# First sub-layer of a two-layer trunk: the first modulation group in two halves, squares of one token tile moved to VectorE

## The chip, the core and the metric

The kernel runs on one NeuronCore of one Trainium2 chip, as one launch. The metric is the device time of the launch in microseconds (us), a median over several runs. The engines are TensorE (PE in the profile, with its weight loads as PEld), VectorE (DVE), ScalarE (ACT), GpSimd (POOL) and SyncE (SP), which issues most loads. Each engine works through its own list of instructions in order and waits at semaphores for the others.

## The reference, cut to what matters

128 context tokens and 256 latent tokens (three tiles of 128 tokens, width 1024) pass through two layers of three sub-layers each. The change is in the start of the first sub-layer alone:

```
m  = (silu(cond) @ mod_w[0] + mod_b[0]).reshape(9, 1024)       # shift = m[0], scale = m[1], for each of two conds
hf = rms_norm(x, g[0]) * (1 + scale) + shift
x  = x + 0.5 * m[2] * rms_norm((silu(hf @ w1g) * (hf @ w1u)) @ w2, g[1])     # w1: 1024 x 5632, w2: 2816 x 1024
```

`rms_norm(x)` needs the sum of squares of each token. `shift` and `scale` need 2048 columns of the modulation weights (8 MB in fp32). All later sub-layers take the same path, but their modulation is computed under the sub-layer before.

## The kernel before

Products in fp32 precision are made of three matmuls in a faster format: each operand is split into a high part and a low rest (`xh`, `xl` for the tokens, `whi`, `wlo` for weights), and `mm3` adds high by high, low by high and high by low (the three matmuls of L445 to L447, one after the other).

`start` holds the whole stretch that is changed. Its steps:

- The tokens arrive as three tiles of 0.5 MB, `x` tile 0, 1, 2. `stat_steps` gives for a tile two squares with an accumulated sum (ScalarE, L331, one for each half of 512 columns), a reciprocal root (a `Sqrt` on ScalarE, L309, and small VectorE steps, in `rstd_of`), and a scaled tile `xn` (half on VectorE, L384, half on ScalarE, L385).
- `transposed` turns `xn` into column blocks on TensorE (L391) and copies them to `xnT` (L765, one half on VectorE, one on ScalarE).
- The modulation vectors come in four groups g of 256 columns of shift and 256 of scale, that is of two column blocks k = 2g and 2g + 1 each. `load(g)` loads two tiles of 1 MB. `mods(g, v)` multiplies one by the conditioning in 8 small matmuls (L788), `rows` copies the result out of PSUM (L796), `vectors` transposes it by 4 matmuls with two columns (L801), and four VectorE instructions (L809, L811) add bias and norm weight.
- `evac(g)` applies scale and shift for both column blocks of a group: `xtmp` on VectorE (L840) and ScalarE (L842), then `xh` (ScalarE, L431) and `xl` (VectorE, L432).
- `products(g, u)` multiplies these blocks by the first three weight units u (gate and up columns, gus 0 and 1): 12 matmuls for a group and unit. Where a number of products is given below, each is one matmul of L445 to L447.

`keep_warm` runs matmuls on the identity with no use for the result; ten stand at the start, ten before the first `evac`. The instructions of this stretch run in the order in which the code emits them on each engine (`order_begin` fixes it). SyncE issues the loads in the order of the code, and a load waits until the eighth load before it has landed. After `start` comes the loop over the other weight units in `ffn`, and then the five further sub-layers; none of that is edited.

Of the kernel before, what the change touches and what calls it, by code (L numbers as in the profile page):

```python
# [26 lines left out]
RS = -0.5  # L27
# [4 lines left out]
HALF_BUFS = 3  # L32
WARM, WARM2 = 10, 10
TAIL = 5


class Trunk:
    def __init__(self, ctx, tc, io):
        self.ctx, self.tc, self.nc, self.io = ctx, tc, tc.nc, io
        nc = self.nc  # L40
# [21 lines left out]
        self.sel = const("sel", [P, 2])  # L62
        nc.gpsimd.dma_start(self.sel, io["sel"])
        self.csT = const("csT", [P, KC, 32])
        nc.vector.memset(self.csT, 0.0)
# [305 lines left out]
    def stat_steps(self, t):  # L371

        nc = self.nc
        st = {}

        square, eps, sums = self.square_steps([self.x[:, t, 0:512], self.x[:, t, 512:1024]])

        def rstd():
            eps()
            st["z"] = self.rstd_of(**sums)  # L380

        def scale(tag="xn"):
# [342 lines left out]
    def start(self, units):  # L725


        nc, io = self.nc, self.io
        with self.tc.tile_pool(name="start", bufs=1, reuse_waits="tile") as tp:
# [13 lines left out]

            load(0)
            for g in range(2):
                for u in range(3):
                    load_part(u, 512 * g, 512 * (g + 1))
                load(g + 1)
            load_part(0, D, 2 * D)
# [24 lines left out]
            def squares(t):  # L774
                for h in (1, 0):
                    stats[t][0](h)

            vec = [self.mod_vec(v) for v in range(2)]
            self.shift[0], self.scale[0] = vec
# [18 lines left out]
            def vectors(g, *vs):  # L798
                po = self.psum(1)
                for i in range(2 * vs[0], 2 * vs[-1] + 2):  # L800
                    nc.tensor.matmul(po[:, 2 * i : 2 * i + 2], rowsof[g][:, i * P : (i + 1) * P], self.sel,  # L801
                                     start=True, stop=True)
                for v in vs:
                    for j in range(2):
                        k = 2 * g + j
                        src = po[:, 4 * v + 2 * j : 4 * v + 2 * j + 2]
                        b = self.mbT[:, 0, v, k : k + 1]
                        if v == 0:
                            nc.vector.tensor_scalar(vec[0][:, :, k], src, b, None, op0=ALU.add)  # L809
                        else:  # L810
                            nc.vector.tensor_scalar(vec[1][:, :, k], src, b, self.nwT[:, 0, k : k + 1],  # L811
                                                    op0=ALU.add, op1=ALU.mult)

            squares(0), stats[0][1]()
            squares(1)
            xn0 = stats[0][2]()
            stats[1][1]()
            squares(2)
            xn1 = stats[1][2]("ptmp")
            nc.vector.tensor_scalar(self.nwT, self.nwT, RS, None, op0=ALU.mult)  # L820
            for j in range(6):
                nc.vector.tensor_scalar(self.mbT[:, j, 1, :], self.mbT[:, j, 1, :], 1.0, None, op0=ALU.add)
            stats[2][1]()
            transposed(0, xn0)
# [11 lines left out]
            def evac(g, between=None):  # L836
                for j in range(2):
                    k = 2 * g + j
# [11 lines left out]

            def products(g, u, gus=(0, 1)):
                for gu in gus:
                    for j in range(2):
                        k = 2 * g + j
# [494 lines left out]
def host_arrays(i):  # L1349
# [12 lines left out]
    first = np.asarray(i["mod_w"])[0, :, 0:2048].reshape(KC, P, 2, 4, 256)  # L1362
    a["mod_first"] = f(first.transpose(3, 2, 1, 0, 4))
    mb = np.asarray(i["mod_b"]).reshape(6, 3, D)
# [86 lines left out]
```

## Time and profile before

| | |
|---|---|
| median of 3 runs | 1422.34 us (1422.31 to 1422.74) |
| profiled execution, its own time | 1423.91 us |
| its span, first to last instruction | 1421.0 us |
| TensorE busy | 1405.4 us (99%) |
| VectorE, ScalarE, GpSimd busy | 1021.1, 614.5, 29.0 us |
| mean granted clock | 0.999 |

The span lies inside the execution's own time; the other 2.9 us are before the first and after the last instruction. A busy TensorE is one with a matmul in flight; at full rate the matmuls of L445 to L447 overlap each other.

### The profile page before, as it was taken

The page shows a single profiled execution, that of the slowest core. Times are in us where ns is not written, and L with a number is a line of the kernel's source. Part 1 is how long each engine was busy: PE and PEld are TensorE (multiplying, and loading weights), DVE is VectorE, ACT ScalarE, POOL GpSimd, SP SyncE. Part 2 cuts the span into 40 slices and gives each one's busy share as a digit, 9 for nine tenths or more (in the row PEclk, how much of TensorE's full clock was granted, in tenths as well). Part 3 has the DMA queues.
Part 4 walks back from the last instruction along what each step waited for, and adds up shares of the span by engine and source line. Part 5 has one row for each costly group of instructions (what it writes and reads, how often), then busy time and mean ns, then how long its engine had stood idle before and what let it go on. Part 6 is the DMA issues. An engine that isn't in the chain of part 4 may idle for free.

```text
span 1421.0 us, 19853 instructions
## 1 busy us (share of the span) xinstructions
PE 1405.4 (99%) x7747; PEld 1287.3 (91%) x7747; DVE 1021.1 (72%) x1798; ACT 614.5 (43%) x1051; POOL 29.0 (2%) x54
## 2 busy tenths in 40 slices
PE   8999999999999999999999999999999999999998
PEld 6999998889888999999889999988886899999886
DVE  5688868578997777986856889887678765555333
ACT  5533332363555633333355333323657663333322
POOL 0000000010000000000000000000100000000000
PEclk9999999999999999999999999999999999999999
DMA  9556555626545246655734566556350334444321
GB/s 372 212 214 259 195 207 221 260 100 247 201 149 199 96 175 235 237 207 182 275 135 153 203 233 241 198 217 251 107 205 30 119 119 152 173 150 178 130 107 45
DMA packets 38958, 262.58 MB, mean 185 GB/s; under 512 B 4816, under 2 KB 4976, under 8 KB 8784
## 3 DMA queue, kind: packets, MB, share of 16 engines
q1 hardware_dynamic: 35424, 243.29, 46.9%
q0 software_dynamic: 3440, 18.02, 3.5%
q8 instruction: 60, 0.98, 0.3%
q14 instruction: 34, 0.28, 0.1%
HBM read 259.01 MB, written 2.29 MB: 184 GB/s over the span
## 4 chain that ended last, share of the span: by engine, by line
PE 93%; DVE 3%; DMA 1%; ACT 1%; issue 1%; DVEq 0%; SPq 0%; ACTq 0%; POOLq 0%
PE psB L445 29%; PE psB L446 29%; PE psB L447 29%; PE psB L391 2%; PE psB L941 1%; PE psB L982 1%; DVE junkv L229 1%; DVE wlo L155 1%; DMA raw<-in_mod_w 1%; DMA csB<-crows 1%; PE psB L788 0%; ACT junk L331 0%; DMA x<-in_x_prompt 0%; PE psB L955 0%; PE psB L801 0%
## 5 line engine op out<-in xcount | busy, mean ns | idle before, releaser
L445 PE MATMUL psB<-xh,whi 128*128 128x384 f32 (+1 forms) x1536 | 517.0, 337 | 0.9 <-ACT qz L1085 0.7
L446 PE MATMUL psB<-xl,whi 128*128 128x384 f32 (+1 forms) x1536 | 512.3, 334 | 0.1
L447 PE MATMUL psB<-xh,wlo 128*128 128x384 f32 (+1 forms) x1536 | 512.0, 333 | 0.0
L155 DVE TENSOR_TENSOR wlo<-raw,whi 128x1024 fp32r<-128x1024 f32 (+2 forms) x286 | 336.6, 1186 | 121.0 <-ACT whi L152 119.2
L152 ACT CAST whi<-raw 128x1024 fp32r<-128x1024 f32 (+1 forms) x275 | 285.6, 1045 | 295.8 <-PE psB L446 132.2
L229 DVE CUSTOM_DVE_ANT_0 junkv<-raw,csB,mbT 128x1024 bf16<-128x1024 f32 x256 | 328.1, 1281 | 8.8 <-DMA csB<-crows 3.7
L445 PEld LDWEIGHTS psB<-xh,whi 128*128 128x128 f32 x1536 | 288.8, 188 | 5.7 <-issue 2.3
L446 PEld LDWEIGHTS psB<-xl,whi 128*128 128x128 f32 x1536 | 288.9, 188 | 1.6 <-DVE xl L432 0.9
L447 PEld LDWEIGHTS psB<-xh,wlo 128*128 128x128 f32 x1536 | 288.8, 188 | 0.0
L445 PE MATMUL psB<-whi,g 128*128 128x512 f32 x384 | 149.9, 390 | 0.0
L447 PE MATMUL psB<-whi,g 128*128 128x512 f32 x384 | 149.4, 389 | 0.0
L446 PE MATMUL psB<-wlo,g 128*128 128x512 f32 x384 | 149.4, 389 | 0.0
L431 ACT CAST g<-gt 128x384 fp32r<-128x384 f32 (+1 forms) x84 | 42.5, 505 | 201.3 <-DVE gt L622 201.3
L622 DVE TENSOR_TENSOR gt<-psB,sil 128x384 f32<-128x384 f32 (+1 forms) x88 | 48.1, 547 | 82.5 <-PE psB L447 74.7
L445 PEld LDWEIGHTS psB<-whi,g 128*128 128x128 f32 x384 | 72.1, 188 | 14.9
L447 PEld LDWEIGHTS psB<-whi,g 128*128 128x128 f32 x384 | 72.1, 188 | 14.9
L446 PEld LDWEIGHTS psB<-wlo,g 128*128 128x128 f32 x384 | 72.1, 188 | 14.7
L432 DVE TENSOR_TENSOR g<-gt,g 128x384 fp32r<-128x384 f32 (+1 forms) x84 | 46.1, 549 | 48.1 <-ACT g L431 48.1
L620 ACT ACTIVATE sil<-psB 128x384 f32<-128x384 f32 (+1 forms) x88 | 42.7, 485 | 86.5 <-PE psB L447 86.5
L445 PE MATMUL psB<-g,g 128*128 128x512 f32 x120 | 46.9, 391 | 0.0
L447 PE MATMUL psB<-g,g 128*128 128x512 f32 x120 | 46.7, 389 | 0.0
L446 PE MATMUL psB<-g,g 128*128 128x512 f32 x120 | 46.7, 389 | 0.0
(227 smaller groups left out, 1410.1 us busy)
## 6 DMA issues: line engine op xcount, KB each, us to landing
raw<-in_ffn_w SPq DMA_DIRECT2D x129, 1024.0 KB, 4.9
raw<-in_mod_w SPq DMA_DIRECT2D x64, 1024.0 KB, 4.9
raw<-in_ev_in SPq DMA_DIRECT2D x10, 1024.0 KB, 4.8
m<-in_mod_first SPq DMA_DIRECT2D x8, 1024.0 KB, 13.1
gate<-gscr POOLq DMA_DIRECT2D x6, 1024.0 KB, 5.0
csB<-crows POOLq DMA_DIRECT2D x4, 1024.0 KB, 7.4
raw<-in_ev_out SPq DMA_DIRECT2D x4, 1024.0 KB, 5.1
raw<-in_od_out SPq DMA_DIRECT2D x4, 1024.0 KB, 4.9
```

Source lines behind the costliest of these rows:

```text
L152: nc.scalar.copy(hi, src)
L155: sub = lambda hi=hi[:, c], lo=lo[:, c], src=src[:, c]: nc.vector.tensor_tensor(lo, src, hi.bitcast(F32), ALU.subtract)
L229: nc.vector.tensor_tensor_reduce(junk[:, :D], self.raw[i][0][:, kk * D : (kk + 1) * D], self.csB[:, c, :], 1.0, self.mbT[:, s, kind, k : k ...
L391: self.nc.tensor.transpose(out, src, self.ident)
L431: self.nc.scalar.copy(hi, src)
L432: sub = lambda: self.nc.vector.tensor_tensor(lo, src, hi.bitcast(F32), ALU.subtract)
L445: nc.tensor.matmul(out, ah, bh, start=first, stop=False)
L446: nc.tensor.matmul(out, ah, bl, start=False, stop=False)
L447: nc.tensor.matmul(out, al, bh, start=False, stop=last)
L620: nc.scalar.activation(sil[:, :n], pg[:, :n], AF.Silu)
L622: nc.vector.tensor_tensor(gt[:, :n], pu[:, :n], sil[:, :n], ALU.mult)
L941: nc.tensor.matmul(sp[:, :384], qk(i, e, t + 1), kk(i, e)[0], start=True, stop=True)
```

## The change

The group g = 0 is loaded as four tiles of 0.5 MB, one for each vector v (shift, scale) and column block j, and computed in two halves: `mods_half`, `rows_half` and `vectors_half` for block 0 stand ahead of the transposes of token tile 2; those for block 1 stand behind the first six products. `evac` and `products` take the column blocks of a group apart by `js`, and the order of products and of the groups 1 and 2 among them is new. The squares of token tile 1 go to VectorE (`square_dve`), with their own sum. Seven small VectorE instructions on norm weights and biases go to GpSimd. The second `keep_warm` is gone.

```diff
+        nc.gpsimd.tensor_scalar(self.nwT, self.nwT, RS, None, op0=ALU.mult)
+        for j in range(6):
+            nc.gpsimd.tensor_scalar(self.mbT[:, j, 1, :], self.mbT[:, j, 1, :], 1.0, None, op0=ALU.add)
...
-            load(0)
-            for g in range(2):
-                for u in range(3):
-                    load_part(u, 512 * g, 512 * (g + 1))
-                load(g + 1)
+            load_half(0)
+            load_part(0, 0, 512)
+            load_half(1)
+            load_part(1, 0, 512)
+            load_part(2, 0, 512)
+            load(1)
+            for u in range(3):
+                load_part(u, 512, 1024)
+            load(2)
...
+            def square_dve(h):
+                junk = self.cp.tile([P, D + 192], BF16, tag="junkv", name=self.name("junkv"))
+                xs = self.x[:, 1, 512 * h : 512 * h + 512]
+                nc.vector.tensor_tensor_reduce(junk[:, 0:512], xs, xs, 1.0 / D, zero, ALU.mult, ALU.add,
+                                               ss1[:, h : h + 1])
...
+            def mods_half(v, j):
+                if v == 0:
+                    sums[0, j] = self.psum(0)
+                for kk in range(2):
+                    for q in range(4):
+                        nc.tensor.matmul(sums[0, j][32 * q : 32 * q + 32, P * v : P * v + P],
+                                         self.csT[:, 2 * q + kk, :], raw0[0, v, j][:, 2 * q + kk, :],
+                                         start=(kk == 0), stop=(kk == 1))
...
-            squares(0), stats[0][1]()
-            squares(1)
+            squares(0), stats[0][3]()
+            square_dve(1)
+            stats[0][1]()
+            stats[2][0](1)
             xn0 = stats[0][2]()
-            stats[1][1]()
-            squares(2)
-            xn1 = stats[1][2]("ptmp")
-            nc.vector.tensor_scalar(self.nwT, self.nwT, RS, None, op0=ALU.mult)
-            for j in range(6):
-                nc.vector.tensor_scalar(self.mbT[:, j, 1, :], self.mbT[:, j, 1, :], 1.0, None, op0=ALU.add)
+            square_dve(0)
+            stats[2][0](0)
+            nc.vector.tensor_tensor(ss1[:, 0:1], ss1[:, 0:1], ss1[:, 1:2], ALU.add)
+            z1 = self.rstd_of(ss1[:, 0:1])
+            xn1 = stats[1][2]("ptmp", z1)
             stats[2][1]()
             transposed(0, xn0)
             xn2 = stats[2][2]()
             transposed(1, xn1)
-            mods(0, 0)
-            rows(0, 0)
+            mods_half(0, 0)
+            mods_half(1, 0)
+            rows_half(0)
+            vectors_half(0)
             transposed(2, xn2)
-            mods(0, 1)
             parts = {0: self.prep(1, "all")}
             parts[0][0]()
-            rows(0, 1)
...
-            vectors(0, 0, 1)
-            keep_warm(0, WARM2)
-            evac(0, parts[0][1])
+            evac(0, parts[0][1], (0,))
+            weights(0, 0)
+            products(0, 0, js=(0,))
+            mods_half(0, 1), mods_half(1, 1), rows_half(1)
             for u in (1, 2):
                 parts[u] = self.prep(1, "all")
                 parts[u][0](), parts[u][1]()
-            for u in range(3):
                 weights(u, 0)
-            products(0, 0)
-            products(0, 1)
+                if u == 1:
+                    vectors_half(1)
+                products(0, u, js=(0,))
+            evac(0, None, (1,))
+            products(0, 0, js=(1,))
             for u in range(3):
                 parts[u][2](), parts[u][3]()
             mods(1, 0), mods(1, 1), rows(1, 0, 1)
-            products(0, 2, (0,))
+            products(0, 1, js=(1,))
             vectors(1, 0, 1)
             evac(1)
-            products(0, 2, (1,))
+            products(0, 2, js=(1,))
+            products(1, 0, (0,))
             mods(2, 0), mods(2, 1), rows(2, 0, 1)
-            products(1, 0)
+            products(1, 0, (1,))
             vectors(2, 0, 1)
```

The host array `mod_first0` holds the first group in the new layout. Line numbers of the changed kernel are some 5 higher at the helpers (L445 to L447 become L450 to L452, L331 becomes L334), and 24 to 56 higher in `start`.

The order of instructions shows the change at three places. The first is ScalarE's list from the first square on, before; `ss_6`, `ss_7` and `ss_8` are the sums of token tiles 0, 1 and 2, and `xn_168` and `xn_186` the scaled tiles 0 and 1:

```order
L331 ACTIVATE junk_149,ss_6_133<-x 128x512
L331 ACTIVATE junk_151,ss_6_133<-x 128x512
L309 ACTIVATE rq_154<-ss_6_133 128x1
L331 ACTIVATE junk_164,ss_7_134<-x 128x512
L331 ACTIVATE junk_166,ss_7_134<-x 128x512
L385 ACTIVATE xn_168<-x,rz_161 128x512
L309 ACTIVATE rq_172<-ss_7_134 128x1
L331 ACTIVATE junk_182,ss_8_135<-x 128x512
L331 ACTIVATE junk_184,ss_8_135<-x 128x512
L385 ACTIVATE xn_186<-x,rz_179 128x512
L309 ACTIVATE rq_197<-ss_8_135 128x1
```

The same stretch of ScalarE's list in the changed kernel, where `xn_182` and `xn_200` are the scaled tiles 0 and 1, and `rv_191` the sum of tile 1 from VectorE:

```order
L334 ACTIVATE junk_163,ss_6_144<-x 128x512
L334 ACTIVATE junk_165,ss_6_144<-x 128x512
L312 ACTIVATE rq_170<-ss_6_144 128x1
L334 ACTIVATE junk_180,ss_8_146<-x 128x512
L390 ACTIVATE xn_182<-x,rz_177 128x512
L334 ACTIVATE junk_187,ss_8_146<-x 128x512
L310 ACTIVATE rq_190<-rv_191 128x1
L390 ACTIVATE xn_200<-x,rz_197 128x512
L312 ACTIVATE rq_204<-ss_8_146 128x1
```

The two squares of tile 1 are gone, and a square of tile 2 stands on either side of the scaling of tile 0, ahead of the root of tile 1.

The second place is TensorE's list around its first products, before; `psB_42` and `psB_43` take the transposes of token tile 2, `m_0_1` is the scale tile of group 0, and `psB_46` collects gate columns of unit 0:

```order
L391 MATMUL psB_42_245<-ident,xn_219 128x128 x4
L391 MATMUL psB_43_246<-ident,xn_219 128x128 x4
L788 MATMUL psB_40_234<-m_0_1_99,csT 32x256 x8
L801 MATMUL psB_52_275<-sel,rows_243 128x2 x4
L771 MATMUL psB_53_284<-ident 128x128 x10
L445 MATMUL psB_46_269<-xh,whi_265 128x384
L446 MATMUL psB_46_269<-xl,whi_265 128x384
L447 MATMUL psB_46_269<-xh,wlo_266 128x384
L445 MATMUL psB_46_269<-xh,whi_265 128x384
L446 MATMUL psB_46_269<-xl,whi_265 128x384
L447 MATMUL psB_46_269<-xh,wlo_266 128x384
```

The same place in the changed kernel, where `psB_44` and `psB_45` take the transposes of token tile 2, `m0h_1` are the two tiles of block 1 (shift, then scale), and `psB_48` and `psB_49` collect the gate and up columns of unit 0:

```order
L855 MATMUL psB_43_260<-sel,rows_258 128x2 x2
L396 MATMUL psB_44_265<-ident,xn_226 128x128 x4
L396 MATMUL psB_45_266<-ident,xn_226 128x128 x4
L450 MATMUL psB_48_280<-xh,whi_277 128x384
L451 MATMUL psB_48_280<-xl,whi_277 128x384
L452 MATMUL psB_48_280<-xh,wlo_278 128x384
L450 MATMUL psB_49_281<-xh,whi_277 128x384
L451 MATMUL psB_49_281<-xl,whi_277 128x384
L452 MATMUL psB_49_281<-xh,wlo_278 128x384
L844 MATMUL psB_56_300<-m0h_1_110,csT 32x128 x8
L844 MATMUL psB_56_300<-m0h_1_112,csT 32x128 x8
L855 MATMUL psB_60_323<-sel,rows_317 128x2 x2
```

The transposes of tile 2 moved behind the small matmuls of `vectors_half(0)`, and 16 small matmuls and two more of `vectors_half(1)` moved from ahead of the first product to behind the sixth.

The third place is TensorE's list behind the vectors of group 1 (the end of the products of group 0 and unit 2, then those of group 1), before; `m_2_0` and `m_2_1` are the tiles of group 2, and `psB_46` is the first bank that takes products of group 1:

```order
L447 MATMUL psB_51_274<-xh,wlo_311 128x384
L788 MATMUL psB_66_396<-m_2_0_114,csT 32x256 x8
L788 MATMUL psB_66_396<-m_2_1_116,csT 32x256 x8
L445 MATMUL psB_46_269<-xh,whi_265 128x384
L446 MATMUL psB_46_269<-xl,whi_265 128x384
L447 MATMUL psB_46_269<-xh,wlo_266 128x384
```

The same place in the changed kernel, with `psB_48` as the first bank of group 1's products:

```order
L452 MATMUL psB_53_285<-xh,wlo_335 128x384
L450 MATMUL psB_48_280<-xh,whi_277 128x384
L451 MATMUL psB_48_280<-xl,whi_277 128x384
L452 MATMUL psB_48_280<-xh,wlo_278 128x384
L450 MATMUL psB_48_280<-xh,whi_277 128x384
L451 MATMUL psB_48_280<-xl,whi_277 128x384
L452 MATMUL psB_48_280<-xh,wlo_278 128x384
L812 MATMUL psB_69_417<-m_2_0_125,csT 32x256 x8
```

Six products of group 1 moved from behind the 16 small matmuls of group 2 to ahead of them.

## Rows read from the trace of the kernel before

**Rows 1.** Stretches: length, busy PE, PEld, DVE, ACT, POOL, granted clock, DMA share, GB/s.

```profile
0.00:18.10 18.10, 12.65 (x104) 10.25 (x105) 9.12 (x39) 13.44 (x30) 2.97 (x10) 1.00 0.89 333
...
20.20:37.90 17.70, 17.70 (x148) 15.00 (x147) 8.95 (x23) 7.09 (x13) 0.00 (x0) 1.00 1.01 414
```

**Rows 2.** Timeline, ScalarE: start, duration, instruction, idle time before it and what ended it.

```profile
6.63 0.63 ACT L331 ACTIVATE junk<-x 128x512 bf16<-128x512 f32 x1
...
10.18 0.70 ACT L385 ACTIVATE xn<-x,rz 128x512 f32<-128x512 f32 x1
...
10.79 0.28 ACT L309 ACTIVATE rq<-ss 128x1 f32<-128x1 f32 x1
...
11.75 0.72 ACT L385 ACTIVATE xn<-x,rz 128x512 f32<-128x512 f32 x1 [0.21 <-DVE rz L322]
...
13.89 0.59 ACT L765 COPY xnT<-psB 128x512 f32<-128x512 f32 x1 [0.95 <-PE psB L391]
...
14.38 0.62 ACT L154 CAST whi<-raw 128x512 fp32r<-128x512 f32 x1
...
16.68 0.60 ACT L842 ACTIVATE xtmp<-xnT,mv,mv 128x256 f32<-128x256 f32 x1 [1.68 <-DVE mv L811]
```

**Rows 3.** Timeline, VectorE, the copy of the first group.

```profile
13.22 0.42 DVE L796 COPY rows<-psB 128x256 f32<-128x256 f32 x1
```

**Rows 4.** Timeline of the issues of loads on SyncE.

```profile
8.23 5.39 SPq L742 DMA_DIRECT2D raw<-in_ffn_w  x3
```

**Rows 5.** Waits of SyncE in the first 24 us: total, times, longest.

```profile
SPq L742 <- DMA x<-in_x_sample: 1.3, 1, 1.3
```

**Rows 6.** Chain that ended last, in order of time: start, duration, what.

```profile
9.55 0.72 ACT junk L331 x2
...
12.77 1.09 PE psB L391 x8
...
13.86 1.00 PE psB L788 x16
...
15.40 0.62 PE psB L801 x4
...
19.92 0.44 PE psB L446
...
20.54 0.17 PE psB L445
```

**Rows 7.** Timeline, TensorE (a small or fp32 matmul counts twice).

```profile
4.17 3.86 PE L771 MATMUL psB<-ident 128*128 128x128 f32 x20 [4.17 <-POOL ident masks.py:199]
...
15.87 2.48 PE L771 MATMUL psB<-ident 128*128 128x128 f32 x20
...
18.47 0.45 PE L446 MATMUL psB<-xl,whi 128*128 128x384 f32 x1
...
23.59 1.93 PE L788 MATMUL psB<-m,csT 128*32 128x256 f32 x32
...
26.61 0.95 PE L801 MATMUL psB<-sel,rows 128*128 128x2 f32 x8
...
28.65 1.93 PE L788 MATMUL psB<-m,csT 128*32 128x256 f32 x32
...
30.51 0.44 PE L445 MATMUL psB<-xh,whi 128*128 128x384 f32 x1
...
32.90 0.95 PE L801 MATMUL psB<-sel,rows 128*128 128x2 f32 x8
```

**Rows 8.** Timeline, ScalarE and VectorE, evacuation of group 1.

```profile
28.80 0.51 ACT L431 CAST xh<-xtmp 128x384 fp32r<-128x384 f32 x1
...
30.79 0.56 DVE L432 TENSOR_TENSOR xl<-xtmp,xh 128x384 fp32r<-128x384 f32 x1 [0.63 <-ACT xh L431]
```

**Rows 9.** Timeline, VectorE, a multiply with a sum.

```profile
65.91 1.28 DVE L229 CUSTOM_DVE_ANT_0 junkv<-raw,csB,mbT 128x1024 bf16<-128x1024 f32 x1 [0.58 <-ACT csB L209]
```

**Rows 10.** Chain that ended last, in the second sub-layer.

```profile
316.09 7.44 DMA csB<-crows
```

More of the change, by code (lines that the diff above doesn't have):

```diff
@@ L32 @@
 HALF_BUFS = 3
-WARM, WARM2 = 10, 10
+WARM = 10
 TAIL = 5
@@ L380, in rstd, with scale @@
             st["z"] = self.rstd_of(**sums)
-        def scale(tag="xn"):
+        def scale(tag="xn", z=None):
+            if z is not None:
+                st["z"] = z
             xn = self.cp.tile([P, D], F32, tag=tag, name=self.name("xn"))
@@ L742, in load_part, with load_half @@
                 nc.sync.dma_start(self.raw[u][0][:, c0:c1], self.unit_src(units[u])[0][:, c0:c1])
-            load(0)
-            for g in range(2):
-                for u in range(3):
-                    load_part(u, 512 * g, 512 * (g + 1))
-                load(g + 1)
+            def load_half(j):
+                for v in range(2):
+                    raw0[0, v, j] = tp.tile([P, KC, P], F32, tag=f"m0h_{v}_{j}", name=f"m0h_{v}_{j}")
+                    nc.sync.dma_start(raw0[0, v, j], io["mod_first0"][j, v])
+            load_half(0)
[7 more added lines that the diff above has]
+            load(2)
             load_part(0, D, 2 * D)
@@ L776, in squares @@
                     stats[t][0](h)
+            zero = self.sp.tile([P, 1], F32, tag="l", name=self.name("l"), bufs=4)
+            nc.vector.memset(zero, 0.0)
+            ss1 = self.sp.tile([P, 2], F32, tag="ss2", name="ss1", bufs=4)
+            def square_dve(h):
[3 more added lines that the diff above has]
+                                               ss1[:, h : h + 1])
             vec = [self.mod_vec(v) for v in range(2)]
@@ L804, in vectors @@
                     for j in range(2):
[L805 to L812, printed above, removed]
@@ L814, in start, with set_vec @@
-            squares(0), stats[0][1]()
-            squares(1)
-            xn0 = stats[0][2]()
-            stats[1][1]()
-            squares(2)
-            xn1 = stats[1][2]("ptmp")
-            nc.vector.tensor_scalar(self.nwT, self.nwT, RS, None, op0=ALU.mult)
-            for j in range(6):
-                nc.vector.tensor_scalar(self.mbT[:, j, 1, :], self.mbT[:, j, 1, :], 1.0, None, op0=ALU.add)
+                        set_vec(v, 2 * g + j, po[:, 4 * v + 2 * j : 4 * v + 2 * j + 2])
+            def set_vec(v, k, src):
+                b = self.mbT[:, 0, v, k : k + 1]
+                if v == 0:
+                    nc.vector.tensor_scalar(vec[0][:, :, k], src, b, None, op0=ALU.add)
+                else:
+                    nc.vector.tensor_scalar(vec[1][:, :, k], src, b, self.nwT[:, 0, k : k + 1],
+                                            op0=ALU.add, op1=ALU.mult)
@@ new lines, in mods_half, with rows_half @@
+            def mods_half(v, j):
+                if v == 0:
+                    sums[0, j] = self.psum(0)
[4 more added lines that the diff above has]
+                                         start=(kk == 0), stop=(kk == 1))
+            def rows_half(j):
+                rowsof[0, j] = tp.tile([P, 256], F32, tag="rowsh", name=self.name("rows"))
+                nc.vector.tensor_copy(rowsof[0, j], sums[0, j][:, 0:256])
@@ new lines, in vectors_half @@
+            def vectors_half(j):
+                po = self.psum(1)
+                for v in range(2):
+                    nc.tensor.matmul(po[:, 2 * v : 2 * v + 2], rowsof[0, j][:, v * P : (v + 1) * P], self.sel,
+                                     start=True, stop=True)
+                for v in range(2):
+                    set_vec(v, j, po[:, 2 * v : 2 * v + 2])
+            squares(0), stats[0][3]()
+            square_dve(1)
+            stats[0][1]()
+            stats[2][0](1)
+            xn0 = stats[0][2]()
@@ L826, in start, with evac @@
             transposed(1, xn1)
-            mods(0, 0)
-            rows(0, 0)
+            mods_half(0, 0)
+            mods_half(1, 0)
+            rows_half(0)
+            vectors_half(0)
             transposed(2, xn2)
-            mods(0, 1)
             parts = {0: self.prep(1, "all")}
             parts[0][0]()
-            rows(0, 1)
             banks = [self.psum(b) for b in (6, 7, 4, 5, 2, 3)]
-            def evac(g, between=None):
-                for j in range(2):
+            def evac(g, between=None, js=(0, 1)):
+                for j in js:
                     k = 2 * g + j
@@ L849, in weights, with products @@
                 ws[u, h] = self.half(units[u], h, ahead=0, hold=True)
-            def products(g, u, gus=(0, 1)):
+            def products(g, u, gus=(0, 1), js=(0, 1)):
                 for gu in gus:
-                    for j in range(2):
+                    for j in js:
                         k = 2 * g + j
@@ L1362, in host_arrays @@
     first = np.asarray(i["mod_w"])[0, :, 0:2048].reshape(KC, P, 2, 4, 256)
-    a["mod_first"] = f(first.transpose(3, 2, 1, 0, 4))
+    first = first.transpose(3, 2, 1, 0, 4)
+    a["mod_first"] = f(first)
+    a["mod_first0"] = f(first[0].reshape(2, P, KC, 2, P).transpose(3, 0, 1, 2, 4))
     mb = np.asarray(i["mod_b"]).reshape(6, 3, D)
```

## The prediction

> **What bounds the kernel now.** I read the stretches first, then the timelines of the first 35 us engine by engine, and the chain of waits last. From 20.2 to 37.9 us TensorE is busy in all 17.70 us [rows 1], and its share of the whole is 99%: once products have begun, what is added to TensorE's list, or what makes it stop, is added to the time. Before 18.1 us TensorE is no bound (12.65 us busy, much of it warm-up matmuls): there a chain of small steps through ScalarE, VectorE and TensorE decides when the first product can start, while the loads keep the DMA engines at 0.89 to 1.01 of full use [rows 1]. So the change has three places to cost or give time: the chain ahead of the first product, the products' order up to the vectors of group 2, and the loads. Behind the vectors of group 2 both lists are the same, and I carry the lag found there to the end.
>
> I place everything against the trace of before: first low-part product (L446, it waits for `xl`) at 18.47, group 1's small matmuls at 23.59, its vectors at 26.61, group 2's vectors at 32.90 [rows 7].
>
> **1. The chain ahead of the first product.** Before, ScalarE goes from the root of tile 0 straight to the squares of tile 1, at 6.63 [rows 2]. Now a square of tile 2 stands there. SyncE's load issue at 8.23 is the one that waited 1.3 us for tokens [rows 4, 5]; it is the fourth load, tile 2, that it needs, so tile 2 lands at 8.2. ScalarE is idle from 6.63 to 8.23: the 1.5 us of squares that it is spared are spent waiting. From there its list is: square, scaling of tile 0, square, root of tile 1. A square and its sum take 0.72 [rows 6], a scaling holds it 0.61 (10.18 to 10.79) [rows 2]: 8.23 + 0.72 + 0.61 + 0.72 = 10.3 for the root of tile 1. VectorE's squares must not be later. Such a multiply with a sum takes 1.28 us for 1024 columns [rows 9]; no row has it at 512, so between half (0.64) and all of it (1.28), and as most VectorE steps scale with the columns I take 0.8. Two of them, with the small steps and the scaling of tile 0 between (0.96, as below, and 0.4), end at 6.6 + 3.0 = 9.6, and two small steps later the root could run at 10.0: hidden, with 0.3 to spare. At 1.28 each the root would be at 10.9; that is an upper bound of +0.6. What is queued behind the first of them, tile 0's scaling, comes 1 us later than before, and TensorE's transposes of tile 0 with it; the end of the chain is tile 2, so this costs nothing.
>
> From a root to the ScalarE half of the scaling it takes 0.96 (10.79 to 11.75) [rows 2]. So tile 1 is scaled at 11.3 and the root of tile 2, which is next, starts at 11.9, against 10.79: 1.1 us late. Behind it VectorE has the same four steps as before (copy, scaling, copy, then the `rows` copy at 13.22 [rows 3]), so `rows_half` copies at 14.3, for 0.42, to 14.75. Two `vectors` matmuls take 0.62 to their result [rows 6]: 15.4, and two vector instructions make 15.8. That is some 0.8 ahead of before (16.6). But it can't be used: TensorE now has the transposes of tile 2 behind `vectors_half(0)`. It is free at 15.2, transposes for 1.09 [rows 6] to 16.3, ScalarE copies (0.5, 13.89 to 14.38), casts weights (0.55 of the 0.62) [rows 2] and only then applies scale and shift, at 17.35 against 16.68. Before, that copy and cast were done while ScalarE waited 1.68 us for the vectors. **First product: 0.7 us later** (0.3 to 1.3).
>
> **2. From the first product to the small matmuls of group 1.** Before 18.47 to 23.59: 5.12 us for 24 products. A product behind a wait takes 0.28 to 0.44, then each 0.17 [rows 6]. Now: the rest of six products 0.98 (0.28 and four of 0.17); the 16 small matmuls of block 1, which were ahead of the first product before; a wait for their result and its copy, 0.2 + 0.42 + 0.1 = 0.7; two `vectors` matmuls 0.4; 18 products 3.1; and a stall of about 0.5, since block 1 needs some 2.9 us from its vectors to `xl` and TensorE has 0.4 + 12 x 0.17 = 2.5 us to do in that time. The small matmuls with 256 columns take 1.86 for a pair of tiles (28.65 to the product at 30.51) [rows 7]. With 128 columns no row shows them: half (0.93) if the columns set their pace, all of it (1.86) if weight loads or issue do. I take 1.3, nearer the half, since the row's matmuls stream four at a time. Sum 0.98 + 1.3 + 0.7 + 0.4 + 3.1 + 0.5 = 7.0: **1.9 us more** (1.5 to 2.4).
>
> **3. From the vectors of group 1 to those of group 2.** 26.61 to 32.90, 6.29 us. Evacuation is fixed by VectorE and ScalarE: `xh` of the first block is cast from 28.80 for 0.51, the last `xl` is made from 30.79 for 0.56, done at 31.35 [rows 8]. Before, TensorE had six products and then group 2's small matmuls (28.65 to 30.51) [rows 7], which don't need `xl`, and so lost about 0.3 us. Now six products of group 1 stand ahead of these, with nothing else to do: the sixth is out at 31.4 + 0.28 + 0.17 = 31.85, the small matmuls last to 33.7, six products more (1.04) to 34.75. That is 34.75 - 32.90: **1.85 us more** (1.6 to 2.0).
>
> **4. What costs nothing.** The ten warm-ups (15.87 for 2.48 us [rows 7]) run while TensorE waits, so their removal gives nothing. The first warm-ups took 3.86 for the same ten matmuls [rows 7], at a granted clock that is recorded as 1.00, the level of 2.4 GHz, in this stretch too [rows 1]. If TensorE slowed like this once more, now that it rests for 2 us ahead of the products, a like stretch would cost 1.4 us. The Trainium skill (TensorE: Matmul & The Clock Gate, What's actually happening) says that the half-rate clock is the default state and that activity releases it; by that a rest could bring it back, and the sum would be 1.4 higher. The trace agrees for the start, where the same matmuls were slower, but shows no fall after it.
>
> The seven GpSimd instructions have their inputs and nobody waits for them until 15.4; on VectorE they lay beside ScalarE's squares. The loads: the first two halves are 1 MB, where the first tile of 1 MB was; the second MB of before was multiplied at 13.86 [rows 6]. At 414 GB/s [rows 1] 1 MB takes 2.5 us, so the first halves are there by 11.4, and wanted at 12.8; the second halves have 0.25 MB more ahead of them, 14.5, and are wanted at 20.1. All later loads have the same bytes ahead. Two more issues on SyncE lie in its waits.
>
> **Sum.** 0.7 + 1.9 + 1.85 = 4.4 us, between 3.4 and 5.7. The profiled execution's own time is 1423.91 us, a span of 1421.0 and 2.9 around it that the change doesn't touch: 1428.3 with the lag. The median of the runs is 1.57 lower, 1422.34, and the forecast for it is **1426.7 us**.
>
> **Rivals.**
> *The front hangs on the loads.* The second MB came just ahead of its use (13.86 [rows 6]); if the first product waited for it, half a group could begin up to 2.5 us sooner, and -2.5 + 1.9 + 1.85 gives +1.2, 1423.5: not slower, as far as this measurement tells (no change means within 0.2%, 2.8 us). It decides if the first low-part product runs before 17.6. Against it: TensorE's list has the transposes of tile 2 in the way and these come late by step 1. The Trainium skill (Perfetto Trace Analysis, DMA Optimizations) says that splitting loads lets some work start sooner where DMA engines are idle; here they are not, as the share of 0.89 and 1.01 shows [rows 1].
> *The lag is given back later.* In the second sub-layer the chain runs through a load of `csB` of 7.44 us at 316.09 [rows 10]. If that load kept its time while TensorE comes 4.4 us later, the lag would vanish: 1422.3 to 1425.1; it takes 1.6 us given back to be no change. Against it: the load is issued when the work before it is done, so it moves with it.
> *TensorE's clock falls* without the second warm-up: 4.4 + 1.4 = 5.8, 1428.1 or some more.
> *The change helps* by over 0.2%: the first product would have to come over 6 us sooner than before; nothing in the trace allows that, bar an error in my reading of the lists.
>
> **How the numbers follow.** Forecast (lag of 3 to 5.4 us) 0.68; slower clock 0.11; loads decide 0.08, given back 0.08, faster 0.05. Slower by over 0.2%: 0.68 + 0.11 = 0.79. Within: 0.16. Faster: 0.05. The range reaches down to 1424.3, where a part of step 2 or 3 is hidden, and up to 1428.5 with the clock.
>
> **What would show it.** Right: ScalarE idle from 6.6 to 8.2; `rows_half` on VectorE at about 14.3; first low-part product at 19.1; about 0.7 us without products behind the small matmuls of block 1; group 1's small matmuls at 26.2, its vectors at 29.2; 2.4 us or so between `vectors` of group 1 and the sixth product beyond what the products take; group 2's vectors at 37.3, and the same lag at 60 us and at the end. Wrong: a first product before 18 us, or small matmuls of group 2 right behind the products, or a lag at 60 us that is gone at 400.

## The result, and the profile after

The changed kernel takes 1431.96 us (median of 4 runs, 1429.63 to 1432.62); the kernel before, beside it, 1422.37 us (1422.31 to 1422.74). The ratio is 1.0063, 95% interval 1.0051 to 1.0074: slower, by 9.6 us. The forecast was 1426.7 us, with a range of 1424.3 to 1428.5: the direction was right and the size was not.

The page of the changed kernel, its span, its engines' busy time and the granted clock in 40 slices of the span:

```profile
span 1430.4 us, 19878 instructions
...
PE 1411.1 (99%) x7759; PEld 1291.4 (90%) x7759; DVE 1021.7 (71%) x1796; ACT 612.6 (43%) x1047; POOL 31.2 (2%) x61
...
PEclk8999999999999999999999999999999999999999
```

TensorE is busy 5.7 us longer than before with nearly the same work, and the first slice of the clock row is an 8. Here is TensorE alone in the stretches of the start (from and to, length, busy and instructions, granted clock, DMA share, GB/s):

```profile
8.00:11.00 3.00, 1.83 (x12) 1.00 1.01 350
11.00:14.50 3.50, 2.88 (x28) 0.57 1.01 389
14.50:18.50 4.00, 2.27 (x32) 0.93 1.04 432
18.50:22.00 3.50, 2.43 (x6) 0.50 1.01 397
22.00:28.50 6.50, 5.95 (x47) 0.50 1.02 418
...
31.00:38.50 7.50, 6.32 (x48) 1.00 0.99 404
38.50:42.00 3.50, 3.50 (x34) 0.54 0.06 23
```

Before, the clock was 1.00 in both stretches of [rows 1], and in the last one here too:

```profile
38.50:42.00 3.50, 3.50 (x40) 1.00 0.55 138
```

Now it is at its lower level, 1.2 GHz, in three stretches: from about 11 to 14.5, from 18.5 to 28.5 and from 38.5 to 42 us. TensorE's timeline shows what that does to single instructions, and where it waits:

```profile
11.62 1.97 PE L396 MATMUL psB<-ident,xn 128*128 128x128 f32 x8 [1.22 <-DVE ss L340]
13.52 1.72 PE L844 MATMUL psB<-m0h,csT 128*32 128x128 f32 x32
...
16.26 1.07 PE L396 MATMUL psB<-ident,xn 128*128 128x128 f32 x8
19.57 0.69 PE L450 MATMUL psB<-xh,whi 128*128 128x384 f32 x1 [2.23 <-ACT xh L436]
20.16 0.69 PE L451 MATMUL psB<-xl,whi 128*128 128x384 f32 x1
...
22.06 1.94 PE L844 MATMUL psB<-m0h,csT 128*32 128x128 f32 x32
...
30.14 1.93 PE L812 MATMUL psB<-m,csT 128*32 128x256 f32 x32
...
33.15 0.95 PE L825 MATMUL psB<-sel,rows 128*128 128x2 f32 x8
...
35.90 0.44 PE L450 MATMUL psB<-xh,whi 128*128 128x384 f32 x1 [0.64 <-ACT xh L436]
36.50 0.45 PE L451 MATMUL psB<-xl,whi 128*128 128x384 f32 x1 [0.15 <-DVE xl L437]
...
38.49 3.42 PE L812 MATMUL psB<-m,csT 128*32 128x256 f32 x32
...
43.13 0.95 PE L825 MATMUL psB<-sel,rows 128*128 128x2 f32 x8
```

Against [rows 7]: the first low-part product is 1.69 us late (20.16), group 1's small matmuls 6.55 (30.14), its vectors 6.54 (33.15), group 2's vectors 10.23 (43.13). These delays mix two things. The rests at 35 us (0.64 and the waits behind it) are the order's. The rest of 2.23 us ahead of the first product is mostly not: the kernel before has one of 1.87 us there once its warm-ups are taken out (e3, below), so what is new is that nothing fills it. The 3.42 us for the same small matmuls of group 2 that took 1.93 before [rows 7] are the clock's.

The lag is carried to the end. The load of the second sub-layer's chain [rows 10] now reads, in the chain of waits:

```profile
326.37 7.15 DMA csB<-crows
```

It ends at 333.52, 10 us later than before (323.53). At the end of the span 9.4 us are left.

ScalarE's part of the front went as described. It waits for token tile 2 where it was spared the squares (against [rows 2]):

```profile
6.70 0.29 ACT L312 ACTIVATE rq<-ss 128x1 f32<-128x1 f32 x1
8.35 0.63 ACT L334 ACTIVATE junk<-x 128x512 bf16<-128x512 f32 x1 [1.36 <-DMA x<-in_x_sample]
...
11.72 0.29 ACT L312 ACTIVATE rq<-ss 128x1 f32<-128x1 f32 x1
```

The root of tile 2 runs at 11.72 (11.9 forecast, 10.79 before). On VectorE the square of 512 columns and the copy of the rows (against [rows 3]) read:

```profile
6.74 0.75 DVE L799 CUSTOM_DVE_ANT_0 junkv<-x,l 128x512 bf16<-128x512 f32 x1 [0.64 <-DMA x<-in_x_sample]
...
15.31 0.42 DVE L850 COPY rows<-psB 128x256 f32<-128x256 f32 x1 [1.06 <-PE psB L844]
```

The square takes 0.75 us (0.8 was assumed). The copy waits 1.06 us for TensorE, whose transposes and small matmuls were at half clock.

### The profile page after: what moved, and what is told of

Same layout as the page of the kernel before. It is cut to its first block, busy times and chain, and to the rows that moved or that the text cites. A ratio compares the mean times of both kernels' runs of the same rounds, so it can differ in the third digit from the quotient of the medians.

```text
span 1430.4 us, 19878 instructions
## 1 busy us (share of the span) xinstructions
PE 1411.1 (99%) x7759; PEld 1291.4 (90%) x7759; DVE 1021.7 (71%) x1796; ACT 612.6 (43%) x1047; POOL 31.2 (2%) x61
## 3 DMA queue, kind: packets, MB, share of 16 engines
q0 software_dynamic: 3440, 18.02, 3.4%
## 4 chain that ended last, share of the span: by engine, by line
PE 93%; DVE 4%; issue 1%; DMA 1%; ACT 1%; SPq 0%; DVEq 0%; ACTq 0%; POOLq 0%
PE psB L450 29%; PE psB L451 29%; PE psB L452 29%; PE psB L396 2%; PE psB L992 1%; DVE junkv L232 1%; PE psB L1033 1%; DVE wlo L158 1%; DMA csB<-crows 0%; PE psB L812 0%; DMA x<-in_x_sample 0%; PE psB L844 0%; PE psB L1006 0%; ACT xh L436 0%; PE psB L1038 0%
## 5 line engine op out<-in xcount | busy, mean ns | idle before, releaser
L450 PE MATMUL psB<-xh,whi 128*128 128x384 f32 (+1 forms) x1536 | 518.4, 338 | 3.5 <-ACT xh L436 3.1
L452 PE MATMUL psB<-xh,wlo 128*128 128x384 f32 (+1 forms) x1536 | 512.9, 334 | 0.0
L450 PEld LDWEIGHTS psB<-xh,whi 128*128 128x128 f32 x1536 | 289.7, 189 | 9.2 <-ACT xh L436 4.0
L452 PEld LDWEIGHTS psB<-xh,wlo 128*128 128x128 f32 x1536 | 289.4, 188 | 0.0
L450 PE MATMUL psB<-whi,g 128*128 128x512 f32 x384 | 149.9, 390 | 0.0
L452 PE MATMUL psB<-whi,g 128*128 128x512 f32 x384 | 149.5, 389 | 0.0
L452 PEld LDWEIGHTS psB<-whi,g 128*128 128x128 f32 x384 | 72.1, 188 | 15.1
L450 PEld LDWEIGHTS psB<-whi,g 128*128 128x128 f32 x384 | 72.1, 188 | 14.8
L450 PE MATMUL psB<-g,g 128*128 128x512 f32 x120 | 46.9, 391 | 0.0
L452 PE MATMUL psB<-g,g 128*128 128x512 f32 x120 | 46.7, 390 | 0.0
```

Of the source, the lines that this page charges most:

```text
L450: nc.tensor.matmul(out, ah, bh, start=first, stop=False)
L452: nc.tensor.matmul(out, al, bh, start=False, stop=last)
```

## The experiments

The theory to test (A): the order costs some 4.4 us, as forecast, and TensorE's clock the rest. Rivals: the order is neutral and all is the clock's (B), the missing warm-ups are all of it (C), or the order costs all of it through waits that I have not found. The runs are in three groups (e1 to e4; e5 to e9; a2 to e11), each on one chip with the kernel before beside it, whose medians there are 1422.07, 1422.38 and 1422.47 us.

| run | median us (range, runs) | ratio to before, 95% |
|---|---|---|
| e1_warm2 | 1427.06 (1426.26 to 1429.98, 4) | 1.0037 (1.0022 to 1.0052) |
| e2_warm_all | 1427.84 (1427.44 to 1428.80, 4) | 1.0040 (1.0025 to 1.0055) |
| e3_before_no_warm2 | 1423.91 (1423.38 to 1424.59, 10) | 1.0012 (1.0003 to 1.0022) |
| e4_group2_first | 1427.30 (1425.40 to 1428.65, 6) | 1.0036 (1.0023 to 1.0049) |
| e5_order_and_warm | 1424.47 (1424.06 to 1426.07, 11) | 1.0014 (1.0005 to 1.0023) |
| e6_both_halves_ahead | 1423.26 (1423.04 to 1424.51, 11) | 1.0007 (0.9998 to 1.0016) |
| e7_front_alone | 1423.51 (1422.87 to 1426.19, 11) | 1.0011 (1.0002 to 1.0020) |
| e9_halves_scalar_squares | 1421.81 (1421.33 to 1422.48, 11) | 0.9996 (0.9987 to 1.0004) |
| a2_changed_again | 1431.24 (1427.72 to 1433.02, 5) | 1.0057 (1.0045 to 1.0070) |
| e1_warm2_again | 1427.03 (1426.07 to 1429.29, 5) | 1.0035 (1.0023 to 1.0048) |
| e10_group2_late_alone | 1424.90 (1424.30 to 1426.38, 11) | 1.0018 (1.0009 to 1.0027) |
| e11_halves_rows_first | 1421.81 (1421.45 to 1422.57, 11) | 0.9995 (0.9986 to 1.0004) |

**Warm-ups back into the changed kernel (e1).**

```diff
+            keep_warm(0, 10)
             evac(0, parts[0][1], (0,))
```

> The changed kernel with the ten warm-up matmuls put back ahead of the first evacuation. Theory A (the new order costs about 4.4 us by itself and the half clock of the changed kernel the rest, in three stretches: about 11 to 14.5, 18.5 to 28.3, 38.5 to 42 us): the middle stretch goes or gets short, the others stay; 15 product matmuls at 0.17 instead of 0.32 us give 2.3 us back and the small matmuls beside them about 1: 1428 to 1429. Theory B (the order costs nothing, the half clock is all of the 9.6 us): the middle stretch is two thirds of it, so 1425 to 1426. Theory C (the missing warm-ups are all of it): 1422.5.

ScalarE's wait for tile 2 and TensorE's timeline of this run at the same places:

```profile
8.22 0.63 ACT L334 ACTIVATE junk<-x 128x512 bf16<-128x512 f32 x1 [1.33 <-DMA x<-in_x_sample]
...
18.88 0.44 PE L451 MATMUL psB<-xl,whi 128*128 128x384 f32 x1
...
19.95 1.08 PE L844 MATMUL psB<-m0h,csT 128*32 128x128 f32 x32
...
25.80 1.93 PE L812 MATMUL psB<-m,csT 128*32 128x256 f32 x32
...
28.82 0.95 PE L825 MATMUL psB<-sel,rows 128*128 128x2 f32 x8
...
31.57 0.44 PE L450 MATMUL psB<-xh,whi 128*128 128x384 f32 x1 [0.65 <-ACT xh L436]
...
37.18 0.95 PE L825 MATMUL psB<-sel,rows 128*128 128x2 f32 x8
```

The clock is 1.00 in every stretch of this profile. So these are the costs of the order alone, against [rows 7]: first low-part product +0.41 (18.88 - 18.47); from there to group 1's small matmuls 6.92 instead of 5.12, +1.80; on to its vectors 3.02, as before; from these to group 2's vectors 8.36 instead of 6.29, +2.07. Together 4.28. What the changed kernel lost on top is 43.13 - 37.18 = 5.95 us: 1.28 up to the first product, 3.06 up to group 1's small matmuls, 1.62 behind its vectors. These are the three stretches at half clock; only 0.13 of the 1.28 is a later landing of tile 2 (8.35 instead of 8.22). The first stretch lies ahead of the warm-ups that were put back, so that its absence here isn't their doing.

The expectation under theory A was missed: it said 1428 to 1429 us with two of the stretches left, and the median is 1427.06 with none left in this profile. What stands of A is its split: the order costs 4.28 us where no clock falls, so that the neutral order (B) and the missing warm-ups alone (C, 1422.5) fall.

**More warm-ups (e2)**: 12 ahead of the transposes of tile 1, 14 ahead of the first product, 8 ahead of group 1's products.

```diff
+            keep_warm(1, 12)
...
+            keep_warm(0, 14)
...
+            keep_warm(0, 8)
```

> The changed kernel with 12 warm-ups ahead of the transposes of tile 1, 14 ahead of the first evacuation and 8 ahead of the six products of group 1 that wait for their evacuation. If these keep the granted clock at 1.00 from 10 to 45 us, only the order is left. Theory A: 1426 to 1427 (lag of 3.4 to 5.4 us, group 2's vectors at 36.5 to 37.8 us). Theory B: 1422 to 1423, group 2's vectors at 33. Theory C: as B.

The clock is again 1.00 throughout; the first low-part product is at 19.96, later than in e1, since the warm-ups stand in TensorE's own list, and group 2's vectors at 38.16. The median is no better than e1's, and both it and those vectors lie above what theory A gave (1427, 37.8). All four runs lie within 1.4 us, at a mean clock of 0.999; the four of e1 spread over 3.7.

**Warm-ups out of the kernel before (e3).**

```diff
-            keep_warm(0, WARM2)
```

> The kernel before without its second ten warm-ups, nothing else changed. Theory A: TensorE then rests from 16 to 18.1 us; if the clock falls for it, the first 24 products run at 0.32 in place of 0.17 us until it rises: 1424.5 to 1426.5; if it doesn't fall, since the stretch ahead is busier than in the changed kernel, 1422.3. Theory C: 1432, as in the changed kernel.

It costs 1.84 us. TensorE's stretches of this run, and its first products:

```profile
14.50:18.50 4.00, 2.12 (x18) 0.93 1.03 429
18.50:22.00 3.50, 3.50 (x10) 0.50 1.01 377
22.00:28.50 6.50, 6.50 (x52) 0.79 1.02 421
```

```profile
17.88 0.65 PE L445 MATMUL psB<-xh,whi 128*128 128x384 f32 x1 [1.87 <-ACT xh L431]
18.47 0.69 PE L446 MATMUL psB<-xl,whi 128*128 128x384 f32 x1
...
25.80 1.93 PE L788 MATMUL psB<-m,csT 128*32 128x256 f32 x32
```

TensorE rests for 1.87 us, and the first low-part product is on time, at 18.47 as in [rows 7]. But the clock falls at about 18 us, the first products run at the lower level, and group 1's small matmuls come 2.21 us late, as do group 2's vectors (35.11). None of the ten runs reaches a mean clock of 0.999, which eleven of the fifteen of the kernel before beside them reach. So the warm-ups, which run while TensorE waits, are worth 1.84 us in the kernel before: just under the range that theory A gave (from 1424.5 us), and far from the 1432 us of theory C.

**Group 2's small matmuls first again, no warm-ups (e4).**

```diff
-            products(1, 0, (0,))
             mods(2, 0), mods(2, 1), rows(2, 0, 1)
-            products(1, 0, (1,))
+            products(1, 0)
```

> The changed kernel with the small matmuls of group 2 back ahead of all products of group 1; nothing else changed. Theory A: step 3's 1.85 us go, and with the rest of TensorE at 35 to 38 us the half-clock stretch behind it (1.5 to 2 us): 1428 to 1428.5. Theory B (order neutral, this rest doesn't cause the fall): 1431 to 1432.

It is 5.2 us above the kernel before on its chip, where the changed kernel was 9.6 above on its own: a gain of about 4.4 us, more than theory A gave (1428 to 1428.5) and more than the 2.07 of step 3. In its profile the clock falls only between about 20 and 27 us. The stretch from 31 to 38.5 has no rests now (7.50 busy of 7.50) and 38.5 to 42 is at 1.00. In the changed kernel the rests of step 3 thus cost twice: by themselves, and by a fall that begins in or behind them (1.62 us; its second profile, below, has the same 9.98 us from vectors to vectors). The rests alone don't bring the fall: e1, e2 and e10 have them too, and their profiles show none. The stretch from 11 to 14.5 is at 1.00 here too, though the edit is behind it; that part of the gain is not the edit's.

**Both (e5)**: the edits of e1 and e4 together.

> The changed kernel with two edits: ten warm-up matmuls ahead of the first product again, and the small matmuls of group 2 ahead of the first products of group 1, as before. Theory A (two separate prices, the order's 4.3 us and the clock's 5 us or more): the clock stays at 1.00, step 3 of the prediction (2.1 us in the run with warm-ups alone) is gone as well, and steps 1 and 2 remain: vectors of group 2 at about 35.1 us, 2.2 behind the kernel before, 1424.4 to 1425.0 us. Theory B (all the loss is the clock's; the order is neutral): as the run with warm-ups alone or 1422.5, with no gain from the order. Theory C (the group 2 order is only a cure for the clock, as in the run without warm-ups): no better than the run with warm-ups alone, 1427.

1424.47, as theory A has it. From group 1's vectors (30.09) to group 2's it takes 6.29 us as before, so step 3 is gone:

```profile
36.38 0.95 PE L825 MATMUL psB<-sel,rows 128*128 128x2 f32 x8
```

The clock did not stay at 1.00 as expected: in its profiled execution the stretch from 11 to 14.5 us was again at 0.56, and the first low-part product at 20.14 (18.88 in e1). That run took 1425.39 us at a mean clock of 0.998; nine of the eleven runs were at 0.999.

**Both halves ahead of the first product (e6)**: as e5, and the small matmuls, rows and vectors of block 1 moved ahead of the first product.

```diff
+            mods_half(0, 1), mods_half(1, 1)
...
-            evac(0, parts[0][1], (0,))
+            evac(0, lambda: (rows_half(1), parts[0][1]()), (0,))
             weights(0, 0)
+            vectors_half(1)
+            evac(0, None, (1,))
+            keep_warm(0, 4)
             products(0, 0, js=(0,))
-            mods_half(0, 1), mods_half(1, 1), rows_half(1)
```

> The changed kernel with the small matmuls and the vectors of block 1 ahead of the first product (so the halves are loaded and multiplied as halves, but both before any product), four warm-up matmuls behind them, and the small matmuls of group 2 ahead of group 1's products. Theory A: steps 2 and 3 are gone, the distance from the first product to group 1's small matmuls is 5.1 us as before, and only step 1 is left: first product 0.4 to 0.9 later than before, 1422.5 to 1423.3 us. If the first product now waits for the halves of block 1 (landing by some 14 us) it is the same. Theory B (squares on VectorE and half loads themselves cost): 1425 or more.

+0.88 in the median, with an interval that holds 1. In the trace step 1 is left: the first low-part product is at 19.36, +0.89. From there to group 1's small matmuls (24.72) it takes 5.36, near the 5.12 of before, so step 2 is gone with the small matmuls between products.

**The front alone (e7)**: in the kernel before, token tile 1's squares on VectorE and the seven small instructions on GpSimd; whole group 0, order and warm-ups as before.

```diff
-            squares(0), stats[0][1]()
-            squares(1)
+            squares(0), stats[0][3]()
+            square_dve(1)
+            stats[0][1]()
+            stats[2][0](1)
             xn0 = stats[0][2]()
...
```

> The kernel before with only the squares of token tile 1 on VectorE (and the seven small instructions on GpSimd that go with them); group 0 whole, order and warm-ups as before. Prediction's step 1 says that ScalarE waits for tile 2 what it was spared, and the root of tile 2 comes about 1.1 us later: first low-part product 0.4 to 1.1 us later than before, 1422.5 to 1423.5 us. Rival (the moved squares relieve ScalarE): first product earlier, 1421.5.

+1.13 in the median, so the move of the squares (with the seven small instructions) is a loss and the rival that it relieves ScalarE falls. A part of it is the clock's: the five runs at a mean clock of 0.999 lie between 1422.87 and 1423.34 us, some 0.8 above the kernel before, the other six at 1423.51 and more. The profiled execution is the slowest of them, 1426.19 us, with TensorE at 0.56 and 0.53 of its clock:

```profile
8.00:11.00 3.00, 1.82 (x13) 1.00 1.03 424
11.00:14.50 3.50, 2.48 (x16) 0.56 0.96 359
14.50:18.50 4.00, 4.00 (x36) 0.53 1.04 430
```

There the first low-part product is at 22.63, 4.16 late. The ten warm-ups stand behind this fall and did not prevent it.

**Halves without the moved squares (e9)**: as e6, but all squares on ScalarE as before, and the vectors of block 0 behind the transposes of tile 2.

> The kernel before with group 0 in halves, both ahead of the first product, squares all on ScalarE as before, the seven small instructions on GpSimd. Column block 0 has its vectors before block 1 does, so its scale and shift can begin 1.5 to 1.8 us earlier than 16.68 us; if the first products follow as early, 1420.3 to 1421.0 us. Rival: the loads or the casts of the first weight unit hold the first product where it was, or group 1's loads (landing at 21.3) hold its small matmuls, and nothing is gained: 1421.8 to 1422.6.

No change, as the rival said: the first low-part product is 0.45 early (18.02), but group 1's vectors at 26.64 are not, because VectorE's copy of group 1's rows stood behind its weight casts. Against e6 it is 1.45 us faster. The two differ in where the squares stand and in the place of those vectors; which of the two gives how much was not separated.

**The copy of the rows ahead of these casts (e11).**

```diff
-            for u in range(3):
-                parts[u][2](), parts[u][3]()
             mods(1, 0), mods(1, 1), rows(1, 0, 1)
+            parts[0][2](), parts[0][3]()
             products(0, 1, js=(1,))
             vectors(1, 0, 1)
             evac(1)
+            for u in (1, 2):
+                parts[u][2](), parts[u][3]()
```

> The run with halves ahead of the first product and squares on ScalarE, and VectorE's copy of group 1's rows ahead of its casts of the second weight halves, which held it for 0.8 us (25.05 to 25.90): vectors of group 1 0.5 earlier, at about 26.2, and of group 2 0.3 to 0.5 earlier, 32.6, unless group 2's second load (28.3) bounds them: 1421.3 to 1421.8 us, within what can be told from no change. Rival (the late casts hold the products of group 2): 1422 or more.

Group 1's vectors come at 25.91, 0.7 early, and then a load holds TensorE:

```profile
29.54 1.07 PE L802 MATMUL psB<-m,csT 128*32 128x256 f32 x16 [0.52 <-DMA m<-in_mod_first]
```

Group 2's second tile is the bound, so little is left of the gain (group 2's vectors at 32.73 instead of 32.90). The medians of e9 and e11 are some 0.6 us below the kernel before, with intervals that hold 1: the best version here can't be told from it.

**The changed kernel and e1 again (a2, e1_warm2_again), on one chip.**

> The changed kernel, not edited, beside the same kernel with ten warm-ups (next run) on one chip. Theory A (4.3 us of order, the rest the clock, and which stretches fall to half differs from execution to execution): times between 1427 and 1433 us whose order follows the mean granted clock, a median near 1431, and in the new profile other stretches at half clock than in the first one, or other ends of them. Rival (a fixed cost of the order that I have not found): the same time in every run, the same waits at the same places whatever the clock.

> The changed kernel with ten warm-ups ahead of the first product, again. Theory A: some executions with no fall, at 1426.3 to 1426.7 us (4.3 above the kernel before), and some with one, 1427 to 1430; the median 3 to 5 us below the changed kernel on this chip. Rival (warm-ups do nothing): no difference beyond 1 us.

The new profile of the changed kernel, TensorE by stretch:

```profile
8.00:11.00 3.00, 1.73 (x12) 1.00 1.02 338
11.00:14.50 3.50, 2.22 (x41) 1.00 1.00 382
14.50:18.50 4.00, 1.77 (x13) 0.94 1.04 432
18.50:22.00 3.50, 3.50 (x38) 0.58 1.02 401
22.00:28.50 6.50, 5.79 (x58) 1.00 1.02 417
...
31.00:38.50 7.50, 6.30 (x44) 0.77 0.98 404
38.50:42.00 3.50, 3.50 (x29) 1.00 0.06 21
```

The same list of instructions, and other falls: none from 11 to 14.5, a short one from 18, and one from about 35 us that ends before 38.5. This execution took 1428.96 us. Over the nine runs of the changed kernel the time goes with the mean granted clock: 1427.72, 1428.96 and 1429.63 us at 0.997; 1431.24 and 1431.64 at 0.994; 1432.28, 1432.45, 1432.62 and 1433.02 at 0.993. A fixed cost that I had missed would not do that. Of the nine runs of e1, the five at 0.999 lie between 1426.07 and 1427.03 us, the other four (0.997 and 0.998) between 1427.42 and 1429.98: ten warm-ups lower the chance of a fall, and don't exclude it. On this chip they gain 4.2 us in the median.

The second profile of e1 shows no fall either, and a first product that is later than in the first profile:

```profile
8.67 0.63 ACT L334 ACTIVATE junk<-x 128x512 bf16<-128x512 f32 x1 [1.50 <-DMA x<-in_x_sample]
```

Its first low-part product is at 19.32, +0.85, and group 2's vectors at 37.62, 4.72 late instead of 4.28. Steps 2 and 3 are the same (6.93 and 8.35 us); the difference is the landing of tile 2, 0.45 later.

**Step 3 alone in the kernel before (e10).**

```diff
+            products(1, 0, (0,))
             mods(2, 0), mods(2, 1), rows(2, 0, 1)
-            products(1, 0)
+            products(1, 0, (1,))
```

> The kernel before with one edit: six products of group 1 ahead of the small matmuls of group 2, as in the changed kernel. Step 3 of the prediction alone: six products at 0.17 us and their wait for the last token block, +1.85 us to the vectors of group 2 and to the end (+2.1 from the run with warm-ups): 1424.0 to 1424.6 us. Theory B (order neutral): 1422.4. If TensorE's clock falls in the stretch of waits, up to 2 us more.

```profile
26.68 0.95 PE L801 MATMUL psB<-sel,rows 128*128 128x2 f32 x8
...
30.03 0.45 PE L446 MATMUL psB<-xl,whi 128*128 128x384 f32 x1 [0.15 <-DVE xl L432]
...
32.03 1.93 PE L788 MATMUL psB<-m,csT 128*32 128x256 f32 x32
...
35.04 0.95 PE L801 MATMUL psB<-sel,rows 128*128 128x2 f32 x8
```

From vectors to vectors 8.36 us, 2.07 more than before, the same as in e1, and +2.43 us in the median, above the range that was expected; the eight runs at a mean clock of 0.999 have a median 2.2 above the kernel before. With e5 (steps 1 and 2, +2.09) the medians make 4.5 us; e1 has 4.6 and 5.0. The parts add up to within half a microsecond.

## Why the prediction was too low

- **Step 1, first product +0.7 (0.3 to 1.3): right.** +0.41 and +0.85 in the two profiles of e1, +0.29 in a2's, where the clock fell only as the products began. The spread is the landing of tile 2: ScalarE's square of it starts at 8.11 (a2), 8.22 and 8.67 (e1), 8.52 (e4), and in these four profiles, where the clock is at 1.00 up to about 18 us, the first low-part product stands 10.65 or 10.66 us behind it. ScalarE's wait, the root at 11.72 and the transposes behind `vectors_half(0)` are as described.
- **Step 2, +1.9 (1.5 to 2.4): right.** 6.92 us instead of 7.0. The 16 small matmuls with 128 columns take 1.08 us, nearer the half (0.93) than the 1.3 that was taken, and the wait for their copy 0.55 instead of 0.7; the other terms were each a little short, so that the sum came out.
- **Step 3, +1.85 (1.6 to 2.0): right in its mechanism, just over its bound.** 2.07 in e1 and e10. The waits for `xh` and `xl` end as counted: in e1 the last low-part product starts 4.80 us behind the vectors (33.62 - 28.82), and 31.4 - 26.61 was forecast. The 0.22 us are in what follows: 0.55 instead of 0.45 to the small matmuls, and 3.01 instead of 2.90 for these and six products.
- **The failed step is "What costs nothing".** It put the ten warm-ups at nothing because they ran on an idle engine; e3 measures 1.84 us for their removal, and putting them back into the changed kernel (e1) gains 4.6 and 4.2 us. And it priced the rival *TensorE's clock falls* at one stretch of 1.4 us, with a chance of 0.11. All nine runs of the changed kernel have a mean clock of 0.997 or less; in its first profile there are three stretches at the lower level, and it comes 5.95 us behind e1. The 1.4 came from ten warm-ups that took 3.86 instead of 2.48 us [rows 7]: a row on how long slow matmuls take, none on how long the clock would stay down or how often it would fall. The long stretch alone, 18.5 to 28.5 us, cost about 3 us, with products at 0.32 instead of 0.17.
- **"This costs nothing" for the later transposes of tile 0 may have been wrong in the same way; it is not shown.** TensorE has less to do from 9 to 11.5 us (1.03 us in the changed kernel, 1.65 before). In three of nine profiles with moved squares (the changed kernel, e5, e7) the next stretch was at 0.56 or 0.57, in none of the five without. But a2 had as little to do (1.06) and no fall.
- **The rivals.** The loads did not decide (the first product was late, not early). Of the lag of 10.23 us at 43 us 0.8 are given back by the end of the span, less than that rival needed.

The sum without the clock was 4.4 us for what e1 measures as 4.28 and 4.72 in its traces; the five runs of e1 at a mean clock of 0.999 have a median of 1426.70 us. That it is so close is partly luck, since step 1 came out lower in the first of these traces and step 3 higher. The forecast was that of the changed kernel without falls, and its range had no room for more than one.

The Trainium skill (TensorE: Matmul & The Clock Gate, What's actually happening) says that half rate is the default state and that activity releases it, and that one and the same kernel was measured with different numbers of slow matmuls at its start. The traces agree, with 0.57 and 1.00 for one stretch of one list of instructions; here it happens behind the start too, after rests of TensorE.

What stays open is what makes the clock fall in one execution and not in the next. TensorE was busy 1.83, 1.82 and 1.81 us of the 3 from 8 to 11 us where a fall followed (changed kernel, e7, e5), and 1.73 and 1.90 where none did (a2, the kernel before). No run here separates these.

## What to carry to other kernels

On an engine whose clock can drop, idle time ahead of the bound stretch is not free: look at what keeps it busy there now, and price its loss by how much work would run at the lower level, with several falls in the range and not one. An order that is to start products early on half of the operands gains nothing where the same engine must then stop for the other half: here it paid to put the independent small matmuls ahead of products that wait. Where a step is taken off an engine, check what it would have waited for next: here ScalarE spent the saved squares waiting for a load.

## What was not expected of the hardware

- One list of instructions gave 1427.72 to 1433.02 us, a spread of 0.4% that goes with the mean granted clock. The 21 runs of the kernel before beside a2 lie between 1421.98 and 1423.34 us.
- 32 entries of small matmuls (each matmul counts twice) took 1.08 us with 128 columns and 1.93 with 256: down to these 0.034 us for an entry, the time went nearly with the columns.
- At the lower clock, products followed each other at 0.32 us and not at 0.17, the small matmuls of group 2 took 3.42 and 3.49 instead of 1.93, and eight entries of transposes 1.97 instead of 1.07.
